# The SSM norm's factors leave the state-space stage's pools: one tile for the sum of squares and the broadcast factors

## The chip, the cores and the metric

The kernel runs on one core of a Trainium2 chip. The time is that of one execution on the device in microseconds. Of the kernel before, three runs gave 1232.15, 1234.88 and 1235.67 us (median 1234.88); one further execution, taken with the hardware profiler, took 1229.0 us.

The core has five engines with queues of their own that work in order: PE (TensorE, matrix products), DVE (VectorE), ACT (ScalarE), POOL (GpSimd), and SP, which here issues the transfers (DMA). Operands live in the on-chip SBUF, matrix products end in PSUM.

## The reference, cut to what matters

One layer of a hybrid decoder: 1024 positions of width 1024, a state-space branch and an attention branch over the same normalised input.

```
h = rmsnorm(x, norm_w) * (1 + scale) + shift
z_ssm, xbc, dt_raw, q, k, v, z_att, f_logit, g_logit = split(h @ w_in)
y_ssm = rmsnorm(ssd(xbc, dt_raw, ...) * silu(z_ssm), ssm_norm_w)     # 16 heads of 64, chunks of 128
y_att = softmax(q k^T * scale + f_cum_q - f_cum_k, causal) v * silu(z_att)   # 8 heads of 128
merged = sigmoid(g_ssm) * (y_ssm @ w_proj_ssm) + sigmoid(g_att) * (y_att @ w_proj_att)
out = rmsnorm(x + gate * (merged @ w_out), final_norm_w)
```

The change concerns the second `rmsnorm`: for each position the mean of the squares over the 1024 state-space channels, its inverse square root, and the product of that factor with the channels.

## The kernel before, in words

All large products are made from operands split into a high and a low part (`split`: a copy by ACT into `hi`, a subtraction by DVE into `lo`), with three partial products for each. Activations lie with channels on the 128 partitions and positions along the row, in eight tiles `hh[k]`, `hl[k]` of 128 x 1024.

After the normalisation and most projections comes the **state-space stage** (pools `sd` in SBUF on the right-hand side and `sdp` in PSUM). It runs over four groups of four heads (`qd`), two halves of the positions (`hf`) and four chunks in each (`ssd_half`). A chunk has a broadcast of decays (`ab`), transposes of the inputs, a state update (`sps`, `st32`, split into `sn`), the outputs in the chunk (`yd`) and those from the carried state (`yo`). After each half, DVE applies skip and gate, ACT squares, and DVE adds to `sacc`, a 128 x 1024 tile that in the end holds, per partition and position, the sum of squares over the channels of that partition. Projections that are independent of it (`FILL`: v, and q and k of several heads) are written between the groups, and the scheduler puts them into gaps on PE.

At the stage's end, eight matmuls with a column of ones add `sacc` over the partitions into `rps`; DVE scales into `rc`, POOL raises to the power -1/2, PE transposes into `rtp`, DVE copies into `rr`, and a DMA stores the 1024 factors in `r_scr`. `rps` and `rtp` are `sp` tiles of the stage's PSUM pool and `sacc` is a tile of its SBUF pool. Then a new pool `m0p` is opened, and a second DMA broadcasts the factors from `r_scr` to the 128 x 1024 tile `rb`. `u_scaled(j)` loads the state-space output `u_scr[j]`, multiplies by `rb` and the weight column, and stores it in `us_scr[j]` for the later projection.

The **attention stage** follows (pools `at` in SBUF, at the place of `sd`, and `atp` in PSUM, at the place of `sdp`): a pool's first tiles wait for the last readers of what lay there before. Before the loop over heads stand, in program order, one `u_scaled`, `qk_slab(0)` (q and k of head 0 are loaded and split) and `v_load(0)`. In head `h`, `attend` makes the logits `lg` for pairs of 128-row blocks, their exponential, transposes `tp`, the product with v in `pv`, and the next head's `qk_slab(h + 1)` is written behind it. For heads whose q or k was not projected earlier that means `c_slab`: two halves of 24 matmuls (lines 111 to 113), each into one tile `mm` of a ring of three that serves the whole program (`mm_tile`), evacuated into `qh`, `ql` or `kh`, `kl` of the pool `at`.

The order on each engine is set once, when the program is built, by a scheduler that plays the program through with its own costs: `attend` and `ssd_half` have raised priorities, and what has no raised priority is drawn ahead into gaps as far as buffers allow. Tiles of one ring are handed out in program order.

Of the kernel before, what the change touches and what calls it, by code (L numbers as in the profile page):

```python
# [24 lines left out]
F32 = mybir.dt.float32  # L25
# [6 lines left out]
P = 128  # L32
S = 1024
# [28 lines left out]
R_C, R_SHIFT, R_SCALE, R_NW, R_SNW, R_BG, R_CB, R_CW = 0, 8, 16, 24, 32, 40, 56, 66  # L62
# [3 lines left out]
def build(ctx, tc, t):  # L66
    nc = tc.nc
    V, A, G, PE, SP = nc.vector, nc.scalar, nc.gpsimd, nc.tensor, nc.sync
# [7 lines left out]
    def f32(ap):  # L76
        return ap.bitcast(F32)

    def ev(name):
        return evp.tile([P, 1028], F32, tag="ev", bufs=4, name=name)  # L80
# [16 lines left out]
    def split(raw, hi, lo, n, eng=V):  # L97
        A.copy(out=hi[:, :n], in_=raw[:, :n])  # L98
        eng.tensor_tensor(out=lo[:, :n], in0=raw[:, :n], in1=f32(hi[:, :n]), op=ALU.subtract)  # L99
        return hi, lo  # L100

    def mm_tile():
        return mmp.tile([P, 512], F32, tag="mm", name="mm")
# [11 lines left out]
    def c_slab(src, slab, xh, xl, evac):  # L115

        units = [unit(src[slab, u], 512) for u in range(2)]
        for hf in range(2):
            ps = mm_tile()
            c_half(hf, units, xh, xl, ps)  # L120
            evac(slice(hf * 512, (hf + 1) * 512), ps)
# [29 lines left out]
    cols = const.tile([P, NROWS], F32, name="cols")  # L151
# [7 lines left out]
    r_scr = dram.tile([8, P], F32, name="r_scr")  # L159
# [174 lines left out]
    def v_slab(pair, dtf=None):  # L334
        vt = []

        def evac(tb, ps):
            per = ps.shape[1]
            g, i = tb // 4, tb % 4
            if i == 0:  # L340
                vt.append(ev("vt")[:, :1024].rearrange("p (i c) -> p i c", i=4))
            A.copy(out=vt[g][:, i:i + per, :], in_=ps[:, :, 0:256])
            if dtf is not None:
                V.tensor_copy(out=dtf[:, tb:tb + per, :], in_=ps[:, :, 256:280])
            if i + per == 4:
                SP.dma_start(out=v_scr[pair][g], in_=vt[g])

        if dtf is not None:
            with tc.issue_after(was["last"].ins):
                t_slab([t["w_v0"][u] for u in range(4)], 280, hh, hl, evac)  # L350
        else:
            t_slab([t["w_v"][pair - 1, u] for u in range(4)], 256, hh, hl, evac)
# [274 lines left out]
            fb()  # L627


    with tc.tile_pool(name="sd", bufs=1, side="right") as sd, \  # L630
            tc.tile_pool(name="sdp", bufs=1, space=PSUM) as sdp:

        def sp():
            return sdp.tile([P, 512], F32, tag="sp", bufs=4, name="sp")
# [115 lines left out]
        def qk_spill(n, h):  # L750
            evac, store = qk_out(n, h)
            c_slab(t["w_c"], (Q0 if n == "q" else K0) + h, hh, hl, evac)
            store()

        fill = [lambda p=p: v_slab(p) for p in (1, 2, 3)] + [lambda a=a: qk_spill(*a) for a in SPILL]
        sacc = sd.tile([P, S], F32, name="sacc")
        for qd in range(4):
            st32, sn = sd.tile([P, 256], F32, tag="st32", bufs=1, name="st32"), None
            for hf in range(2):
# [7 lines left out]
                for i in range(2):  # L767
                    j = 2 * qd + i
# [10 lines left out]
                    SP.dma_start(out=u_scr[j][:, hs], in_=y)  # L779
            for f in FILL[qd]:  # L780
                fill[f]()
        rps = sp()
        for tb in range(8):
            PE.matmul(rps[:, 2 * tb:2 * tb + 1], lhsT=sacc[:, tb * P:(tb + 1) * P], rhs=ones[:, 0:1],
                      start=True, stop=True)
# [1 line left out]
        V.tensor_scalar(out=rc, in0=rps[:, 0:16].rearrange("p (a two) -> p a two", two=2)[:, :, 0],  # L787
                        scalar1=1.0 / 1024, scalar2=4 * EPS, op0=ALU.mult, op1=ALU.add)
        G.tensor_tensor(out=rc, in0=rc, in1=mhalf, op=ALU.pow)  # L789
        rtp = sp()  # L790
        PE.transpose(out=rtp[0:8, 0:P], in_=rc, identity=ident)
        rr = const.tile([8, P], F32, name="rr")
        V.tensor_copy(out=rr, in_=rtp[0:8, 0:P])
        SP.dma_start(out=r_scr, in_=rr)


    LO, HI = slice(0, 512), slice(512, 1024)
    rctx, finx = ExitStack(), ExitStack()
    m0p = rctx.enter_context(tc.tile_pool(name="m0p", bufs=1, side="right"))
    rb = m0p.tile([P, S], F32, tag="rb", bufs=1, name="rb")  # L800
    SP.dma_start(out=rb, in_=r_scr.rearrange("(o c) l -> o (c l)", o=1).broadcast_to([P, S]))

    def u_scaled(j):
        ut = ev("ut")
        SP.dma_start(out=ut[:, :S], in_=u_scr[j])
        V.scalar_tensor_tensor(out=ut[:, :S], in0=ut[:, :S], scalar=cols[:, R_SNW + j:R_SNW + j + 1], in1=rb,
                               op0=ALU.mult, op1=ALU.mult)
        SP.dma_start(out=us_scr[j], in_=ut[:, :S])

# [157 lines left out]
    with tc.tile_pool(name="at", bufs=1, side="right") as at, \  # L967
            tc.tile_pool(name="atp", bufs=1, space=PSUM) as atp:

        def qk_slab(h):  # L970
            qh, ql, kh, kl = (at.tile([P, S], F32R, tag=n, bufs=2, name=n) for n in ("qh", "ql", "kh", "kl"))
            def q_evac(hs, ps):
                A.activation(out=qh[:, hs], in_=ps, func=AF.Copy, scale=-QSCALE)
                V.scalar_tensor_tensor(out=ql[:, hs], in0=ps, scalar=-QSCALE, in1=f32(qh[:, hs]),
                                       op0=ALU.mult, op1=ALU.subtract)

            def k_evac(hs, ps):
                A.copy(out=kh[:, hs], in_=ps)
                V.tensor_tensor(out=kl[:, hs], in0=ps, in1=f32(kh[:, hs]), op=ALU.subtract)
            for n, slab, evac, hi, lo in (("q", Q0 + h, q_evac, qh, ql), ("k", K0 + h, k_evac, kh, kl)):  # L980
                if (n, h) in SPILL + PSPILL:
                    qt = ev("qt")
                    SP.dma_start(out=qt[:, :S], in_=qk_scr[n, h])
                    split(qt, hi, lo, S)
                else:
                    c_slab(t["w_c"], slab, hh, hl, evac)
            return qh, ql, kh, kl
# [6 lines left out]
        def v_load(pair):  # L994
            vh, vl = [], []
            for g in range(2):
                vt = ev("vt")[:, :1024].rearrange("p (i c) -> p i c", i=4)
                SP.dma_start(out=vt, in_=v_scr[pair][g])
                vh.append(at.tile([P, 4, 256], F32R, tag="vh", bufs=3, name="vh"))
                vl.append(at.tile([P, 4, 256], F32R, tag="vl", bufs=3, name="vl"))  # L1000
                split(vt, vh[g], vl[g], 4)
            return vh, vl
# [55 lines left out]
            SP.dma_start(out=o_scr[h], in_=zg[:, :S])  # L1058

        prep = iter(range(8))  # L1060
        for _ in range(PREP[-1]):
            u_scaled(next(prep))
        qkt = qk_slab(0)
        vv = v_load(0)
        for h in range(AH):
            if h == HCLOSE:
                hctx.close()
                fin = finx.enter_context(tc.tile_pool(name="fin", bufs=1))
            zg = z_load(h)
            with tc.high_priority(offset=APRI):  # L1070
                attend(h, qkt, vv, zg)
            if h < AH - 1:
                if h % 2:
                    vv = v_load((h + 1) // 2)
                qkt = qk_slab(h + 1)
            if h in EARLY:
                early(EARLY[h])
                if 1 in EARLY[h]:
                    ub = b_quads(us_scr, (12, 22))
            for _ in range(PREP[h]):  # L1080
                u_scaled(next(prep))
# [167 lines left out]
```

## Time and profile before

| | |
|---|---|
| three runs, median (lowest to highest) | 1234.88 us (1232.15 to 1235.67) |
| the profiled execution | 1229.0 us, its span 1227.2 us |
| PE busy | 1162.5 us, 95% of the span |
| DVE busy | 969.8 us, 79% |
| ACT busy | 626.2 us, 51% |
| POOL busy | 87.2 us, 7% |
| end of the last sum into `sacc` | 728.7 us |
| first logits of attention | 733.8 us |
| first multiplication by `rb` | 742.2 us |

Times within the span count from its start. Rows of single instructions show start, duration, engine, line, operation, and in brackets how long the engine stood idle before it and what ended that. Matmuls overlap: the distance from one start to the next is what one costs, its duration is longer. A row with "x8" stands for eight that follow each other, with the time they took together. The rows themselves are shown where the prediction uses them.

### The profile page before, as it was taken

How to read it: one execution, taken by the hardware profiler on the slowest of the kernel's cores; microseconds unless marked ns; L12 is line 12 of the kernel's file. 1: busy time of each engine (PE TensorE's matmuls, PEld its weight loads, DVE VectorE, ACT ScalarE, POOL GpSimd, SP SyncE). 2: the span in 40 equal slices, each digit the busy share in tenths (PEclk: the TensorE clock that was granted, in tenths of full speed). 3: DMA queues.
4: the chain of work that ended last, by engine and by line, in shares of the span. 5: the costliest groups of instructions: out<-in, count | busy, mean ns of one | idle time of the engine just before them, and what ended most of it. 6: DMA issues, size and time to landing. Idle time of an engine off the chain costs nothing.

```text
span 1227.2 us, 18314 instructions
## 1 busy us (share of the span) xinstructions
PE 1162.5 (95%) x6206; PEld 975.1 (79%) x6206; DVE 969.8 (79%) x1990; ACT 626.2 (51%) x1252; POOL 87.2 (7%) x152
## 2 busy tenths in 40 slices
PE   4999899999999999999999989999988998999997
PEld 3797688778877788998888768888877886788875
DVE  6879687887987785589999987664677968989967
ACT  5555344353442344777776633453456654454455
POOL 2000000000000000000000002222322220000001
PEclk9999999999999999999999989999999999999999
DMA  8442442655384756546646658422246526955333
GB/s 350 178 155 98 165 164 79 229 188 190 115 291 167 243 206 223 207 134 205 207 149 199 205 185 304 157 88 89 87 162 208 182 77 239 334 181 180 103 95 146
DMA packets 104122, 219.67 MB, mean 179 GB/s; under 512 B 11818, under 2 KB 19420, under 8 KB 103004
## 3 DMA queue, kind: packets, MB, share of 16 engines
q1 hardware_dynamic: 104028, 218.50, 52.8%
q8 instruction: 49, 0.80, 0.3%
q14 instruction: 45, 0.37, 0.1%
HBM read 154.85 MB, written 63.61 MB: 178 GB/s over the span
## 4 chain that ended last, share of the span: by engine, by line
PE 71%; DVE 14%; DMA 8%; issue 3%; ACT 3%; POOL 0%; SPq 0%; POOLq 0%; DVEq 0%; ACTq 0%
PE pp L492 6%; PE pp L495 6%; PE pp L494 6%; PE pv L1054 4%; PE mm L492 4%; PE mm L494 4%; PE mm L495 4%; PE lg L1023 3%; PE mm L112 3%; PE mm L111 3%; PE mm L113 3%; DMA ab<-a_scr 2%; PE tp L1044 2%; PE mm L908 2%; PE mm L906 2%
## 5 line engine op out<-in xcount | busy, mean ns | idle before, releaser
L98 ACT CAST wh<-wr 128x512 fp32r<-128x512 f32 (+1 forms) x214 | 130.4, 620 | 159.6 <-PE mm L494 27.9
L99 DVE TENSOR_TENSOR wl<-wr,wh 128x512 fp32r<-128x512 f32 (+1 forms) x214 | 145.8, 689 | 47.3 <-ACT wh L98 46.1
L112 PE MATMUL mm<-hl,wh 128*128 128x512 f32 x288 | 116.9, 406 | 0.0
L111 PE MATMUL mm<-hh,wh 128*128 128x512 f32 x288 | 115.5, 406 | 0.1
L113 PE MATMUL mm<-hh,wl 128*128 128x512 f32 x288 | 114.7, 399 | 0.0
L138 PE MATMUL mm<-wh,hl 128*128 128x256 f32 (+1 forms) x256 | 73.7, 289 | 0.0
L136 PE MATMUL mm<-wh,hh 128*128 128x256 f32 (+1 forms) x256 | 73.2, 288 | 0.0
L137 PE MATMUL mm<-wl,hh 128*128 128x256 f32 (+1 forms) x256 | 73.1, 286 | 0.0
L1029 ACT ACTIVATE pr<-pr,sm 128x1024 f32<-128x1024 f32 (+3 forms) x64 | 50.0, 781 | 44.9 <-DVE sm L1028 38.0
L1047 ACT CAST pth<-tp 128x512 fp32r<-128x512 f32 (+1 forms) x80 | 42.4, 542 | 52.7 <-PE tp L1044 44.1
L1024 DVE CUSTOM_DVE_ANT_0 pr<-lg,fb 128x512 f32<-128x512 f32 (+1 forms) x96 | 51.6, 552 | 17.8 <-PE lg L1023 12.2
L112 PEld LDWEIGHTS mm<-hl,wh 128*128 128x128 f32 x288 | 54.9, 191 | 10.8 <-DVE hl L303 0.9
L111 PEld LDWEIGHTS mm<-hh,wh 128*128 128x128 f32 x288 | 54.5, 191 | 10.9 <-ACT hh L302 0.9
L113 PEld LDWEIGHTS mm<-hh,wl 128*128 128x128 f32 x288 | 54.8, 190 | 10.1
L683 ACT ACTIVATE ab<-ab,acs 128x128 f32<-128x128 f32 x128 | 41.0, 391 | 36.5 <-DMA ab<-a_scr 32.7
L1032 POOL TENSOR_SCALAR pr<-pr,sm 128x1024 f32<-128x1024 f32 (+3 forms) x64 | 52.0, 813 | 83.1 <-DVE sm L1031 65.9
L1048 DVE TENSOR_TENSOR ptl<-tp,pth 128x512 fp32r<-128x512 f32 (+1 forms) x80 | 49.9, 631 | 10.0 <-ACT pth L1047 9.7
L789 POOL TENSOR_TENSOR rc<-rc,mhalf 128x8 f32<-128x8 f32 x1 | 1.6, 1647 | 703.9 <-DVE rc L787 703.9
L1054 PE MATMUL pv<-pth,vh 128*128 128x256 f32 (+1 forms) x160 | 45.2, 282 | 4.9 <-DVE zg L1057 4.0
L98 ACT CAST sh<-sr 128x512 fp32r<-128x512 f32 x57 | 34.0, 620 | 30.3 <-PE pp L494 15.0
L137 PEld LDWEIGHTS mm<-wl,hh 128*128 128x128 f32 x256 | 48.2, 189 | 0.2
L138 PEld LDWEIGHTS mm<-wh,hl 128*128 128x128 f32 x256 | 48.2, 189 | 0.1
(399 smaller groups left out, 3507.6 us busy)
## 6 DMA issues: line engine op xcount, KB each, us to landing
wr<-w_c SPq DMA_DIRECT2D x116, 256.0 KB, 3.4
wa<-w_ada SPq DMA_DIRECT2D x8, 1024.0 KB, 11.4
g_scr<-gt SPq DMA_DIRECT2D x16, 512.0 KB, 4.1
ab<-a_scr SPq DMA_DIRECT2D x32, 256.0 KB, 3.6
gt<-g_scr SPq DMA_DIRECT2D x32, 256.0 KB, 3.9
wr<-w_ps SPq DMA_DIRECT2D x28, 256.0 KB, 2.9
wr<-w_pa SPq DMA_DIRECT2D x28, 256.0 KB, 2.8
wr<-so SPq DMA_DIRECT2D x28, 256.0 KB, 2.7
```

Source lines behind the costliest of these rows:

```text
L98: A.copy(out=hi[:, :n], in_=raw[:, :n])
L99: eng.tensor_tensor(out=lo[:, :n], in0=raw[:, :n], in1=f32(hi[:, :n]), op=ALU.subtract)
L111: PE.matmul(ps, lhsT=hi[:, cs], rhs=xh[k][:, hs], start=(k == 0), stop=False)
L112: PE.matmul(ps, lhsT=hi[:, cs], rhs=xl[k][:, hs], start=False, stop=False)
L113: PE.matmul(ps, lhsT=lo[:, cs], rhs=xh[k][:, hs], start=False, stop=(k == 7))
L136: PE.matmul(o, lhsT=xh[k][:, ts], rhs=hi[:, cs], start=(k == 0), stop=False)
L137: PE.matmul(o, lhsT=xh[k][:, ts], rhs=lo[:, cs], start=False, stop=False)
L138: PE.matmul(o, lhsT=xl[k][:, ts], rhs=hi[:, cs], start=False, stop=(k == 7))
L492: PE.matmul(ps, lhsT=f[0][:, w], rhs=xh[:, hs], start=(first and k == 0), stop=False, skip_group_check=True)
L494: PE.matmul(ps, lhsT=f[0][:, w], rhs=xl[:, hs], start=False, stop=False, skip_group_check=True)
L495: PE.matmul(ps, lhsT=f[1][:, w], rhs=xh[:, hs], start=False, stop=(k == 3), skip_group_check=True)
L1054: PE.matmul(pv[:, o0:256], lhsT=x[kb // 4][:, kb % 4, vs], rhs=y[:, d:d + m], start=(kb == 0 and i == 0), stop=(kb == 2 * qq + 1 and i == 2))
```

## The change

`sacc` moves into `m0p`, which is now opened ahead of the state-space stage and stays until the factors are used. The computation of the factors becomes `norm_factors`, written behind `qk_slab(0)` and `v_load(0)`, outside the stage's pools; its two PSUM tiles are `mm` tiles. The factors are broadcast back into `sacc`, and `rb` is gone. The first `u_scaled` is written behind that.

```diff
+    rctx, finx = ExitStack(), ExitStack()
+    m0p = rctx.enter_context(tc.tile_pool(name="m0p", bufs=1, side="right"))
+    sacc = m0p.tile([P, S], F32, name="sacc")
 
     with tc.tile_pool(name="sd", bufs=1, side="right") as sd, \
...
-        sacc = sd.tile([P, S], F32, name="sacc")
         for qd in range(4):
...
-        rps = sp()
+
+    LO, HI = slice(0, 512), slice(512, 1024)
+    def norm_factors():
+        rps = mm_tile()
         for tb in range(8):
             PE.matmul(rps[:, 2 * tb:2 * tb + 1], lhsT=sacc[:, tb * P:(tb + 1) * P], rhs=ones[:, 0:1],
                       start=True, stop=True)
...
         G.tensor_tensor(out=rc, in0=rc, in1=mhalf, op=ALU.pow)
-        rtp = sp()
+        rtp = mm_tile()
         PE.transpose(out=rtp[0:8, 0:P], in_=rc, identity=ident)
         rr = const.tile([8, P], F32, name="rr")
         V.tensor_copy(out=rr, in_=rtp[0:8, 0:P])
         SP.dma_start(out=r_scr, in_=rr)
-
-
-    LO, HI = slice(0, 512), slice(512, 1024)
-    rctx, finx = ExitStack(), ExitStack()
-    m0p = rctx.enter_context(tc.tile_pool(name="m0p", bufs=1, side="right"))
-    rb = m0p.tile([P, S], F32, tag="rb", bufs=1, name="rb")
-    SP.dma_start(out=rb, in_=r_scr.rearrange("(o c) l -> o (c l)", o=1).broadcast_to([P, S]))
+        SP.dma_start(out=sacc, in_=r_scr.rearrange("(o c) l -> o (c l)", o=1).broadcast_to([P, S]))
 
     def u_scaled(j):
...
-        V.scalar_tensor_tensor(out=ut[:, :S], in0=ut[:, :S], scalar=cols[:, R_SNW + j:R_SNW + j + 1], in1=rb,
+        V.scalar_tensor_tensor(out=ut[:, :S], in0=ut[:, :S], scalar=cols[:, R_SNW + j:R_SNW + j + 1], in1=sacc,
...
         prep = iter(range(8))
+        qkt = qk_slab(0)
+        vv = v_load(0)
+        norm_factors()
         for _ in range(PREP[-1]):
             u_scaled(next(prep))
-        qkt = qk_slab(0)
-        vv = v_load(0)
```

Lines behind the stage's head shift by five at most: the sums over the partitions are line 784 before and 791 now, the transpose of the factors 791 and 798, the logits 1023 and 1024, the scaling 806 and 807.

Three places show how the scheduler's order moves. In the rows, `sp` and `mm` are PSUM tiles, `hh_231` to `hh_238` and `hl_239` to `hl_246` the eight tiles of the normalised input, and `wh`, `wl` a split weight.

TensorE at the end of the state-space stage, before: the last projections ahead of the sums, the transpose and the first logits.

```order
L111 MATMUL mm<-hh_238,wh 128x512
L112 MATMUL mm<-hl_246,wh 128x512
L113 MATMUL mm<-hh_238,wl 128x512
L784 MATMUL sp<-ones,sacc 128x1 x4
L791 MATMUL sp<-ident,rc 8x128
L1023 MATMUL lg<-kh,qh 128x512
L1023 MATMUL lg<-kl,qh 128x512
L1023 MATMUL lg<-kh,ql 128x512
```

The same place now:

```order
L733 MATMUL sp<-m_7147,xr 64x128 x12
L791 MATMUL mm<-ones,sacc 128x1 x4
L744 MATMUL sp<-ch_4525,sn 128x128
L745 MATMUL sp<-cl_4527,sn 128x128
L744 MATMUL sp<-ch_4525,sn 128x128
L745 MATMUL sp<-cl_4527,sn 128x128
L791 MATMUL mm<-ones,sacc 128x1 x4
L1024 MATMUL lg<-kh,qh 128x512 x2
L1024 MATMUL lg<-kl,qh 128x512
```

and a few rows on:

```order
L1024 MATMUL lg<-kl,qh 128x512
L1024 MATMUL lg<-kh,ql 128x512
L798 MATMUL mm<-ident,rc 8x128
L111 MATMUL mm<-hh_231,wh 128x512
L112 MATMUL mm<-hl_239,wh 128x512
L113 MATMUL mm<-hh_231,wl 128x512
```

Counted over the whole order, 72 of the 96 projection matmuls of head 1 stood ahead of the first logits, between the chunks of the last half; now none stands there, and the first one follows the transpose of the factors. Both orders have the same number of projections behind them again 216 projections after the first logits now (144 before).

VectorE at the same seam, before:

```order
L773 TENSOR_TENSOR ys<-ys,zt 128x512 x2
L778 TENSOR_TENSOR sacc<-sacc,zt 128x512 x2
L787 TENSOR_SCALAR rc<-sp 128x8
L99 TENSOR_TENSOR ql<-qt,qh 128x1024
L99 TENSOR_TENSOR kl<-qt,kh 128x1024
L793 COPY rr<-sp 8x128
L99 TENSOR_TENSOR vl<-vt,vh 128x1024
L974 SCALAR_TENSOR_TENSOR ql<-mm,qh 128x512 x2
L979 TENSOR_TENSOR kl<-mm,kh 128x512
L1024 ISA pr,sm<-lg,fb 128x512
```

and now:

```order
L782 TENSOR_TENSOR sacc<-sacc,zt 128x512 x2
L99 TENSOR_TENSOR ql<-qt,qh 128x1024
L794 TENSOR_SCALAR rc<-mm 128x8
L99 TENSOR_TENSOR kl<-qt,kh 128x1024
L99 TENSOR_TENSOR vl<-vt,vh 128x1024 x2
L1025 ISA pr,sm<-lg,fb 128x512
L1025 ISA sm 128x1
L1025 ISA pr,sm<-lg,fb 128x512
L1025 ISA sm 128x1
L800 COPY rr<-mm 8x128
```

`rc` moves behind the split of q, the copy `rr` behind two readouts of logits, and the three evacuations of head 1's projections (lines 974 and 979) leave this place. The first multiplication by the factors stands behind four readouts now, and behind two before.

TensorE in head 0, at its last logits, before and now:

```order
L1023 MATMUL lg<-kl,qh 128x128
L1023 MATMUL lg<-kh,ql 128x128
L1054 MATMUL pv<-pth,vh 128x256
L1054 MATMUL pv<-pth,vl 128x256
L1054 MATMUL pv<-ptl,vh 128x256
```

```order
L1024 MATMUL lg<-kh,ql 128x128
L111 MATMUL mm<-hh_233,wh 128x512
L112 MATMUL mm<-hl_241,wh 128x512
L113 MATMUL mm<-hh_233,wl 128x512
L111 MATMUL mm<-hh_234,wh 128x512
L112 MATMUL mm<-hl_242,wh 128x512
```

Sixteen projections stand now between these logits and the product with v, where none stood.

## The prediction

> **What bounds the kernel now.** I read four views in this order: the engine shares and the chain that ended last, a table by stage around the place of the change, the instructions of TensorE and VectorE there, and the waits.
>
> From the page of the profile, the first two shares and the chain:
>
> ```profile
> span 1227.2 us, 18314 instructions
> PE 1162.5 (95%) x6206; PEld 975.1 (79%) x6206; DVE 969.8 (79%) x1990; ACT 626.2 (51%) x1252; POOL 87.2 (7%) x152
> PE 71%; DVE 14%; DMA 8%; issue 3%; ACT 3%; POOL 0%; SPq 0%; POOLq 0%; DVEq 0%; ACTq 0%
> ```
>
> TensorE works 1162.5 of 1227.2 us. All matmuls are the same before and after, so the question is only where its 64.7 us of idle time grow or shrink. By stage (the columns are length, busy time and count of PE, weight loads, DVE, ACT, POOL, then granted clock, DMA share, GB/s):
>
> ```profile
> 702.00:727.00 25.00, 24.43 (x155) 20.13 (x153) 24.14 (x59) 8.42 (x18) 0.00 (x0) 1.00 0.44 143
> 727.00:736.50 9.50, 4.13 (x16) 3.21 (x16) 7.00 (x11) 5.21 (x8) 2.23 (x3) 0.65 0.72 254
> 736.50:798.00 61.50, 59.11 (x327) 50.88 (x326) 41.25 (x98) 25.23 (x49) 14.41 (x23) 1.00 0.66 230
> 798.00:880.00 82.00, 81.90 (x497) 72.25 (x495) 48.33 (x138) 39.33 (x83) 22.46 (x41) 1.00 0.26 91
> 880.00:960.00 80.00, 73.24 (x418) 62.54 (x416) 58.87 (x153) 44.20 (x88) 22.32 (x36) 0.98 0.47 159
> ```
>
> The last stretch of the state-space stage (702 to 727) has DVE at 24.14 of 25 us: it is set by VectorE, and TensorE is full as well, at 24.43. The seam (727 to 736.5) leaves PE over half idle. After it attention is set by TensorE: 59.11 of 61.5, then 81.90 of 82 us, with DVE at two thirds or less. What fills TensorE in the DVE-bound tail is shown by the largest of its groups there (there are three alike, one for each partial product):
>
> ```profile
> L111 PE MATMUL mm<-hh,wh 128*128 128x512 f32 x25 | 10.0, 400 | 0.0
> ```
>
> They are projections of head 1's q and k, which belong to attention and run here for nothing, under VectorE.
>
> **The change part by part.** The factors' two PSUM tiles move from the stage's own pool into the ring of three `mm` buffers, which those projections use too, and stand in it ahead of head 1. The order shows what comes of it: before, 72 of head 1's 96 projection matmuls stand ahead of the first logits; now none does, they begin only behind the transpose of the factors. Counting the projections on TensorE, both orders are even again after the 144 that follow the first logits before (about 798 us), which become 216. No arithmetic is added or removed.
>
> *Cover lost.* The price of one such matmul is its distance to the next when they stand back to back, not its modelled duration:
>
> ```profile
> 707.38 0.39 PE L111 MATMUL mm<-hh,wh 128*128 128x512 f32 x1
> ...
> 710.15 0.39 PE L111 MATMUL mm<-hh,wh 128*128 128x512 f32 x1
> ```
>
> Between these two lie twelve steps in 2.77 us, 0.231 us each. 72 x 0.231 = 16.6 us of TensorE work leave a stretch where they cost nothing and land in one where TensorE is full. That is +16.6 us, unless holes take it up.
>
> *The tail itself.* Does it end sooner? Its VectorE queue:
>
> ```profile
> 717.64 0.68 DVE L99 TENSOR_TENSOR wl<-wr,wh 128x512 fp32r<-128x512 f32 x1
> 718.36 0.42 DVE L741 TENSOR_TENSOR ys<-sp,eb 128x256 f32<-128x256 f32 x1
> ...
> 720.63 0.69 DVE L99 TENSOR_TENSOR wl<-wr,wh 128x512 fp32r<-128x512 f32 x1
> 721.35 0.42 DVE L99 TENSOR_TENSOR sn<-st,sn 64x256 fp32r<-64x256 f32 x1
> 721.80 0.42 DVE L741 TENSOR_TENSOR ys<-sp,eb 128x256 f32<-128x256 f32 x1
> 722.26 0.85 DVE L744 TENSOR_TENSOR ys<-sp,ys 64x256 f32<-64x256 f32 x2
> ...
> 727.25 1.49 DVE L778 TENSOR_TENSOR sacc<-sacc,zt 128x512 f32<-128x512 f32 x2
> ```
>
> The two weight splits (0.72 us each by the next start) go to attention, since the projections no longer free their buffers: -1.4 us at most. Against that, the last state split `sn` now stands right ahead of the multiplication `L741` that needs its matmuls; before, 1.3 us of other work lay between (721.80 to 723.14). I give back 0.9 us for that round trip and take -0.5 us. Bounds: -1.4 us, and +3 us if TensorE, now mostly idle here, answers at half rate (below). Behind the lost cover nothing else hides the tail's wait: TensorE simply stands.
>
> *The seam.* Before, qh's split and the first logits wait for the factors:
>
> ```profile
> 728.79 1.05 PE L784 MATMUL sp<-ones,sacc 128*128 128x1 f32 x8 [2.18 <-DVE sacc L778]
> 731.82 0.38 PE L791 MATMUL sp<-ident,rc 128*8 128x128 f32 x1 [1.99 <-POOL rc L789]
> 733.80 0.77 PE L1023 MATMUL lg<-kh,qh 128*128 128x512 f32 x1 [1.60 <-DMA fb<-f_scr]
> 736.50 0.49 PE L111 MATMUL mm<-hh,wh 128*128 128x512 f32 x1
> 730.12 1.65 POOL L789 TENSOR_TENSOR rc<-rc,mhalf 128x8 f32<-128x8 f32 x1 [703.91 <-DVE rc L787]
> 730.07 1.04 ACT L98 CAST qh<-qt 128x1024 fp32r<-128x1024 f32 x1 [2.26 <-DVE rc L787]
> 731.15 1.23 DVE L99 TENSOR_TENSOR ql<-qt,qh 128x1024 fp32r<-128x1024 f32 x1 [1.11 <-ACT qh L98]
> 732.29 1.22 DVE L99 TENSOR_TENSOR kl<-qt,kh 128x1024 fp32r<-128x1024 f32 x1
> 733.43 0.27 DVE L793 COPY rr<-sp 8x128 f32<-8x128 f32 x1
> ```
>
> The tail's sums end at 728.74. The logits start at 733.80, right behind the copy `rr` (733.70), the last reader of the stage's PSUM pool: 5.06 us, of which 1.05 + 0.38 are work, so 3.6 us idle. Now the pools close with the tail, at T. qh is split T to T+1.0 and kh to T+2.1 on ACT, ql to T+2.3 and kl to T+3.6 on DVE (with `rc` in between); the first two logit matmuls can start at T+2.1, the others at T+3.6. Work in that time is 1.05 us and two logit matmuls of 0.45 (six took 733.80 to 736.50), so TensorE is idle about 1.6 us: -2.0 us. The factor chain moves behind the logits: pow done at T+4.2, transpose at T+6, the copy after two logit readouts at T+7.7. Bounds 0 (another load, such as fb's, still decides) and -3.3 us, the lead that the second logit readout gets.
>
> *The moved scaling.* The broadcast and the `u_scaled` multiplications behind it get later:
>
> ```profile
> 733.90 0.33 SPq L794 DMA_DIRECT2D r_scr<-rr x1
> 738.54 0.32 SPq L801 DMA_DIRECT2D rb<-r_scr x1
> 742.16 2.48 DVE L806 SCALAR_TENSOR_TENSOR ut<-ut,cols,rb 128x1024 f32<-128x1024 f32 x2 [1.94 <-DMA rb<-r_scr]
> ```
>
> From the copy's end to the first multiplication it was 8.5 us (733.7 to 742.16), so it now starts at T+16.2 instead of 13.4 us after the tail. VectorE reaches it after four logit readouts, near T+12, and stands 4 us. Behind it wait block 6's minimum, its exponential, two more multiplications, q's evacuation and the reciprocal; the probabilities are ready about T+22. TensorE comes to their transposes after 64 projections (64 x 0.231 = 14.8) and twelve logit matmuls (2.3) from T+6, at T+23. So I price it at nothing: the projections hide it, with 1 us to spare; without the cover it costs those 4 us. On SP the w_c loads of later heads now queue behind the `us_scr` stores, but q1, k1 and the first half of q2 are split in the tail already, so no projection starves.
>
> *Holes that take the work.* Between 736.5 and 798 TensorE waits once, and later for VectorE:
>
> ```profile
> PE pv L1054 <- DVE zg L1057: 2.2, 1, 2.2
> PE lg L1023 <- DVE sm L1024: 4.0, 3, 2.9
> ```
>
> The first (at 772) lies between head 0's last logits and its values; 16 projections now stand there, 3.7 us, so it fills: -2.2 us. The others lie past 880, behind the point where both orders agree; the work ahead of them moves as one, so they stay.
>
> **The sum:** +16.6 - 0.5 - 2.0 - 2.2 = +11.9 us on the profiled execution's 1229.0 us (span 1227.2), 1240.9. The median of the runs, 1234.88, is 5.9 us above that execution; I add the difference to it: 1246.8, and name 1246.5.
>
> A rule of the Trainium skill speaks against the change as well. The row first: the clock was 0.65 over the seam, and its logit matmuls took 0.45 us each against 0.231. "TensorE: Matmul & The Clock Gate", Part 1, says that half rate is the default and that roughly a 3.4 us window of activity lifts it. The trace agrees in size (2.7 us slow); whether a sparse tail counts as idle no row shows. By the rule the sum would be that of the second rival.
>
> **The rivals.** (1) *Faster.* If attention is set not by TensorE but by the chain of logits, exponential and values, its earlier start carries to the end: -3.3 at the seam and -0.5 in the tail, 1231. For it: the seam's wait is real. Against it: 81.90 of 82 us busy, and one wait of TensorE from 736.5 to 880. It decides only if the 72 matmuls find holes: 16.6 us, where the rows show 2.2 before 880 and 6.8 to 960. Chance 5%. (2) *A slow tail.* Without projections the tail has 24.43 - 16.6 = 7.8 us of matmuls in 25. If its clock falls to half, as at the seam, the groups that VectorE waits for double:
>
> ```profile
> 716.45 0.52 PE L711 MATMUL sp<-xr,bt 128*128 128x256 f32 x3
> 716.80 0.88 PE L728 MATMUL sp<-m,xr 128*64 128x128 f32 x12
> ...
> 721.54 0.88 PE L728 MATMUL sp<-m,xr 128*64 128x128 f32 x12
> 722.25 0.27 PE L739 MATMUL sp<-ch,sn 128*128 128x128 f32 x1
> ```
>
> States take 0.35, outputs 0.71 and the carried part some 0.45 us (four matmuls of the same kind), by their starts: 1.5 us more a chunk, half of it exposed over four chunks, +3. It decides from the point where VectorE has gaps. If the scaling also stands in the way, +4 more: 1250 to 1254. Chance 20%. (3) *Later holes take part.* If half the 6.8 us idle of 880 to 960 is a fixed cost of loads, the sum falls to +8: 1243 or less; with all of it and the clean tail, +4: 1239. Chance 20%. (4) *Nothing moves*, all holes and the seam together cancel the cover: 1235. Chance 5%. The forecast has 50%.
>
> **How the numbers follow.** The range takes the forecast, rival 3 and most of rival 2: 1239 to 1253. This kernel's runs tell 0.3%, 3.7 us, from no change. Faster is rival 1, 5%; same is rival 4 and the lowest tenth of 3, 7%; slower the rest, 88%.
>
> **What would show it.** After the change TensorE should be near 35% busy in the last 25 us of the state-space stage, with no projection ahead of the first logits, and busy without pause from there past the end of head 1. The first logits should start 2 to 3.6 us behind the last `sacc` sum; the first scaling 16 us behind it. The forecast is wrong if TensorE has idle time in heads 0 to 2 that a trace of before doesn't show, or if the tail shrinks by more than 2 us.

## The result, and the profile after

The changed kernel's median over five runs is 1244.27 us (1242.27 to 1249.23), against 1235.67 us (1232.15 to 1237.89) for the kernel before in the same session: a ratio of 1.008, 95% interval 1.0057 to 1.0102. That is 7.0 to 12.6 us more. In a second session the unaltered change gave 1248.14 against 1236.65, ratio 1.0096 (1.007 to 1.0122).

The profiled execution of the change took 1249.23 us, with a span of 1247.5. Some 6 us of that had already gathered ahead of the place of the change, compared with the first profile of before. So the stretches below are shifted by 6.5 us, and the parts are compared from landmark to landmark.

The table by stage after the change (length, then busy time and count of PE, weight loads, DVE, ACT, POOL, then granted clock, DMA share, GB/s): the last 25 us of the state-space stage, the seam, the first 10 us of logits, then the rest to the point where both orders agree, and beyond.

```profile
708.50:733.50 25.00, 13.10 (x83) 11.28 (x81) 22.58 (x57) 6.96 (x16) 0.00 (x0) 0.60 0.37 122
733.50:738.20 4.70, 1.87 (x8) 1.78 (x8) 2.58 (x4) 2.98 (x5) 0.00 (x0) 0.50 0.52 159
738.20:748.20 10.00, 9.66 (x30) 7.08 (x31) 5.53 (x12) 3.12 (x4) 5.15 (x5) 0.70 0.78 295
748.20:821.00 72.80, 71.74 (x399) 61.73 (x398) 45.03 (x104) 28.94 (x59) 14.97 (x26) 1.00 0.53 188
821.00:900.00 79.00, 79.00 (x467) 69.49 (x466) 45.80 (x127) 36.00 (x75) 19.91 (x36) 1.00 0.26 91
```

The tail has 83 matmuls where it had 155, TensorE is busy in half of it instead of all, and its clock has fallen to 0.60. VectorE is still nearly full. Attention is full on TensorE as before. The groups of TensorE in the same tail show what is left: the state-space matmuls and, of the 25 projections of each kind, one at its start (lines 733, 744 and 745 are 728, 739 and 740 before; lines of the stage shift by up to five, those of the norm's factors by seven):

```profile
L733 PE MATMUL sp<-m,xr 128*64 128x128 f32 x48 | 5.4, 289 | 3.3 <-DVE st L722 3.3
L744 PE MATMUL sp<-ch,sn 128*128 128x128 f32 x8 | 3.1, 395 | 4.8 <-DVE sn L99 4.8
L745 PE MATMUL sp<-cl,sn 128*128 128x128 f32 x8 | 3.0, 381 | 0.0
L111 PE MATMUL mm<-hh,wh 128*128 128x512 f32 x1 | 0.4, 444 | 0.0
```

The seam after, by instruction of TensorE, ACT and VectorE:

```profile
735.45 1.87 PE L791 MATMUL mm<-ones,sacc 128*128 128x1 f32 x8 [5.68 <-DVE sacc L782]
738.24 1.22 PE L1024 MATMUL lg<-kh,qh 128*128 128x512 f32 x2 [0.92 <-ACT kh L98]
741.63 0.41 PE L798 MATMUL mm<-ident,rc 128*8 128x128 f32 x1
741.70 0.78 PE L111 MATMUL mm<-hh,wh 128*128 128x512 f32 x1
736.19 1.04 ACT L98 CAST qh<-qt 128x1024 fp32r<-128x1024 f32 x1 [1.72 <-DMA u_scr<-ys]
729.80 0.42 DVE L746 TENSOR_TENSOR ys<-sp,eb 128x256 f32<-128x256 f32 x1 [1.67 <-PE sp L745]
733.91 1.49 DVE L782 TENSOR_TENSOR sacc<-sacc,zt 128x512 f32<-128x512 f32 x2
743.13 0.27 DVE L800 COPY rr<-mm 8x128 f32<-8x128 f32 x1
751.79 1.28 DVE L807 SCALAR_TENSOR_TENSOR ut<-ut,cols,sacc 128x1024 f32<-128x1024 f32 x1 [2.10 <-DMA sacc<-r_scr]
```

The sums end at 735.40, the logits start 2.84 us later (before: 5.06), and the first projection follows the transpose of the factors, as its order says. TensorE waits in the tail for VectorE's states (4.8 + 3.3 us) and 5.68 us for the last sum.

A second profile of each kernel was taken later. The table gives, for every profiled execution that follows, the stretches between five landmarks: U, the second square that starts a sum (before anything the change moves); E, the start of the last addition to `sacc`; G, the first logits; F, the last matmul of line 111, which belongs to the last projections; and the end of the span. The starts come from the groups of these tiles in each trace.

| us | U to E | E to G | G to F | F to end | U to end |
|---|---|---|---|---|---|
| before, first profile | 143.1 | 5.8 | 176.9 | 316.5 | 642.3 |
| before, second profile | 145.5 | 5.7 | 179.3 | 317.2 | 647.7 |
| change, first profile | 143.9 | 3.5 | 193.1 | 316.2 | 656.7 |
| change, second profile | 144.4 | 3.5 | 192.3 | 317.1 | 657.3 |
| tiles in attention's ring | 142.8 | 4.3 | 178.1 | 318.0 | 643.2 |
| before, with mm tiles | 145.5 | 10.6 | 187.6 | 317.0 | 660.7 |
| factors behind head 1 | 145.2 | 4.2 | 184.9 | 317.6 | 651.9 |
| before, one tile | 144.5 | 5.8 | 180.7 | 317.3 | 648.3 |
| change, 72 matmuls left out | 143.6 | 3.6 | 178.3 | 316.7 | 642.2 |
| before, 72 matmuls left out | 144.6 | 6.4 | 174.3 | 317.0 | 642.3 |
| change, 72 matmuls added | 145.2 | 3.5 | 191.6 | 317.2 | 657.5 |

The loss stands in one column: from the first logits to the last projection the change takes 13 to 16 us more, the seam gives back 2.2, and the two other columns differ by no more than they do among executions of one kernel.

### The profile page after: what moved, and what is told of

Its sections match the earlier page's. It is cut to its first block, busy times and chain, and to the rows that moved or that the text cites. A ratio compares the mean times of both kernels' runs of the same rounds, so it can differ in the third digit from the quotient of the medians.

```text
span 1247.5 us, 18316 instructions
## 1 busy us (share of the span) xinstructions
PE 1173.9 (94%) x6206; PEld 983.7 (79%) x6206; DVE 972.7 (78%) x1990; ACT 626.6 (50%) x1252; POOL 87.9 (7%) x152
## 4 chain that ended last, share of the span: by engine, by line
PE 45%; DVE 11%; DMA 8%; ACT 3%; issue 2%; SPq 0%; POOL 0%; POOLq 0%; DVEq 0%; ACTq 0%
PE pv L1055 4%; DMA ab<-a_scr 3%; PE lg L1024 3%; PE mm L111 2%; PE mm L112 2%; PE mm L113 2%; PE tp L1045 2%; PE pp L492 2%; PE pp L494 2%; PE pp L495 2%; PE mm L907 2%; PE mm L909 2%; PE mm L908 2%; PE pp L909 1%; PE pp L1167 1%
## 5 line engine op out<-in xcount | busy, mean ns | idle before, releaser
L136 PEld LDWEIGHTS mm<-wh,hh 128*128 128x128 f32 x256 | 48.1, 189 | 0.2
```

Of the source, the lines that this page charges most:

```text
L136: PE.matmul(o, lhsT=xh[k][:, ts], rhs=hi[:, cs], start=(k == 0), stop=False)
```

## The experiments

**The unaltered kernels again**, for second profiles.

> The changed kernel unaltered, for a second profile beside those of its variants. Cover theory: +7 to +13 us against before; the 6.5 us that the first profile was already late before the first instruction that the change moves are chance of that execution and differ here.

Measured: 1248.14 us, ratio 1.0096 (1.007 to 1.0122). The landmark U came at 590.8 us in the first profile of the change and at 589.1 in the second, against 584.9 and 586.6 for before: over all executions of the table above it lies between 584.9 and 590.8, although TensorE's order is the same up to there. The lateness goes with the clock at the program's start. From 20 to 150 us, first profile of before, then of the change:

```profile
20.00:150.00 130.00, 120.76 (x626) 100.37 (x626) 106.80 (x237) 65.12 (x115) 2.43 (x4) 1.00 0.46 165
20.00:150.00 130.00, 119.38 (x606) 99.53 (x607) 105.88 (x235) 62.74 (x111) 2.44 (x4) 0.97 0.45 163
```

In this stretch the clock was 1.00 in the four executions with U at 584.9 to 587.3, and 0.96 or 0.97 in the seven with U at 588.3 to 590.8. One of the seven is the kernel before with mm tiles, whose pools are untouched, so the lateness is taken as chance of the execution and left out by counting from U. That the change has no part in it is not shown: all six executions of versions made from the change are among the seven.

> The kernel before unaltered, for a second profile. The first one was taken from an execution of 1229.0 us, below all timed runs of it. From one landmark ahead of the change (the second square that starts a sum, at 584.9 us) to the end it took 642.3 us, and the one-tile variant, whose TensorE order is the same, 648.3. If that execution was a quick one, this one takes 644 to 650 from the landmark, and the surplus lies in waits of attention or in its clock; if it was typical, 641 to 643.

Measured: from the landmark to the end 647.7 us. The first profile of before was a quick execution, as this expectation supposed. Of the 5.4 us, 2.4 lie in U to E, whose cause stays open, and 2.4 in G to F. For the latter one cause can be seen here (a second, the clock behind the seam, is shown further on). In both profiles TensorE waits about 2 us in head 0 for VectorE (`pv` for `zg`). In the first the clock stays up behind the hole, in the second it does not. The stages of 10 us behind the hole, first profile, then second:

```profile
773.80:783.80 10.00, 10.00 (x55) 8.49 (x55) 7.00 (x16) 4.52 (x10) 1.84 (x4) 1.00 0.50 182
```

```profile
777.80:787.80 10.00, 10.00 (x49) 8.79 (x48) 6.42 (x15) 3.53 (x8) 1.42 (x4) 0.83 0.46 175
```

**One thing undone: the factors' tiles in another ring.**

```diff
-        rps = mm_tile()
+        rps = atp.tile([P, 512], F32, tag="tp", bufs=2, name="tp")
...
-        rtp = mm_tile()
+        rtp = atp.tile([P, 512], F32, tag="tp", bufs=2, name="tp")
```

> The changed kernel with one thing undone: the two PSUM tiles of the factors come from attention's ring for transposes instead of the mm ring. All 72 projections of head 1 stand ahead of the first logits again. Cover theory: the loss is gone and the earlier seam stays, 0 to 4 us faster than before (about -2), so 8 to 14 us faster than the change. Rival, the scaling by the factors in VectorE's way: it is as late as in the change, so most of the loss stays, +5 us or more against before. Rival, the place of the one tile in SBUF or the longer-lived pool: +6 us stay.

Measured: 1232.21 us against 1237.96, ratio 0.9962 (0.9945 to 0.9979): 2.6 to 6.8 us faster than before. With the projections back in the tail the whole loss is gone, although the scaling still starts 15.1 us behind the last sum (16.4 in the change) and the tile is the same. TensorE's tail is nearly full again, and the stretch of head 0 in which before has its hole shows none:

```profile
708.50:733.50 25.00, 22.52 (x142) 19.05 (x140) 22.30 (x51) 6.67 (x14) 0.00 (x0) 0.96 0.47 154
765.40:775.40 10.00, 10.00 (x64) 8.94 (x63) 7.74 (x16) 6.13 (x14) 2.65 (x5) 1.00 0.79 295
```

This version beats both kernels. Its gain over before, 4.7 us by the ratio, is a little above the 0 to 4 expected. Against the second profile the table shows 1.4 us of it at the seam and 1.2 in G to F; 2.7 lie in U to E, which differs by as much among executions. The hole is gone from G to F, but TensorE waits 1.0 us there for the evacuation of `ql`, and the half rate of the seam goes on for 9.8 us behind the first logits.

**One part alone: mm tiles in the kernel before.**

```diff
-        rps = sp()
+        rps = mm_tile()
...
-        rtp = sp()
+        rtp = mm_tile()
```

> The kernel before with one part of the change alone: the two PSUM tiles of the factors are mm tiles; everything else, the pools, the place in the program and the two SBUF tiles, as before. Cover theory: the tail has no projections again, 18 come between the transpose of the factors and the first logits; the seam keeps its old waits. 72 x 0.231 = 16.6 us, less 18 x 0.231 = 4.2 us that may fit into the seam's wait and less 2.2 us for the hole in head 0: +8 to +14 us against before. Rivals (scaling, place of the tile): those parts are as before, so 0 to +2 us.

Measured: 1248.1 us, ratio 1.0099 (1.0075 to 1.0122), +9 to +15 us. These two lines alone make the loss, without any of the rest of the change. TensorE waits as long for the last sum as in the change, and then for the factors as before:

```profile
PE mm L784 <- DVE sacc L778: 5.7, 1, 5.7
PE mm L791 <- POOL rc L789: 2.0, 1, 2.0
```

**The other part alone: one tile for sum and factors.**

```diff
+    rctx, finx = ExitStack(), ExitStack()
+    m0p = rctx.enter_context(tc.tile_pool(name="m0p", bufs=1, side="right"))
+    sacc = m0p.tile([P, S], F32, name="sacc")
...
     with tc.tile_pool(name="sd", bufs=1, side="right") as sd, \
...
-        sacc = sd.tile([P, S], F32, name="sacc")
...
-    rctx, finx = ExitStack(), ExitStack()
-    m0p = rctx.enter_context(tc.tile_pool(name="m0p", bufs=1, side="right"))
-    rb = m0p.tile([P, S], F32, tag="rb", bufs=1, name="rb")
-    SP.dma_start(out=rb, in_=r_scr.rearrange("(o c) l -> o (c l)", o=1).broadcast_to([P, S]))
+    SP.dma_start(out=sacc, in_=r_scr.rearrange("(o c) l -> o (c l)", o=1).broadcast_to([P, S]))
...
-        V.scalar_tensor_tensor(out=ut[:, :S], in0=ut[:, :S], scalar=cols[:, R_SNW + j:R_SNW + j + 1], in1=rb,
+        V.scalar_tensor_tensor(out=ut[:, :S], in0=ut[:, :S], scalar=cols[:, R_SNW + j:R_SNW + j + 1], in1=sacc,
```

> The kernel before with the other part of the change alone: one tile, outside the stage's pool, for the sum of squares and for the broadcast factors; the computation of the factors stays where it was, with the stage's PSUM tiles. TensorE's order is as before. Cover theory: within 1 us of before. Rival, the tile's place: +3 to +8 us.

Measured: 1238.5 us, ratio 1.0019 (1.0002 to 1.0036), 0.2 to 4.5 us more. That is not the loss, but it is not clearly nothing either; the profile (648.3 us from the landmark, 647.7 in the second of before) shows no place for it, and at 1236.02 us it is one of the quickest of its twelve executions. Neither the expected 1 us nor the lower end of the rival's 3 to 8 us is excluded. Against the rival speaks that the version with the tiles in attention's ring has the same tile and is quicker than before. It stays open.

**The factors behind head 1's projections.**

```diff
         vv = v_load(0)
-        norm_factors()
-        for _ in range(PREP[-1]):
-            u_scaled(next(prep))
         for h in range(AH):
...
+            if h == 0:
+                norm_factors()
+                u_scaled(next(prep))
             for _ in range(PREP[h]):
```

> The changed kernel with the factors written behind head 1's projections instead of ahead of them, so that their two mm tiles come later in the ring. 72 projections stand ahead of the logits again, the factors come some 20 us later still. Cover theory: -1 to -4 us against before, as with the other ring, whatever the factors' lateness. Rival, late scaling: slower than the change, +10 us or more against before.

Measured: 1242.32 us, ratio 1.004 (1.0023 to 1.0058). The expectation missed: the cover is back, and it is still slower than before, though faster than the change; the rival's +10 us is not reached either. Here the late scaling does hurt. VectorE stands for the broadcast and for the loads, and what it owes attention comes late; TensorE waits and its clock falls behind that. VectorE's waits from 758 to 790 us, one such scaling ahead of the split `ptl` that TensorE waits for, the wait of TensorE, and the stage of 10 us around it:

```profile
DVE ut L807 <- DMA ut<-u_scr: 5.3, 2, 3.2
DVE ut L807 <- DMA sacc<-r_scr: 2.6, 1, 2.6
```

```profile
781.02 1.28 DVE L807 SCALAR_TENSOR_TENSOR ut<-ut,cols,sacc 128x1024 f32<-128x1024 f32 x1 [2.03 <-DMA ut<-u_scr]
782.96 0.39 PE L1055 MATMUL pv<-ptl,vh 128*128 128x256 f32 x1 [2.74 <-DVE ptl L1049]
```

```profile
778.20:788.20 10.00, 7.25 (x41) 6.52 (x40) 6.02 (x14) 4.30 (x9) 1.23 (x4) 0.83 0.88 281
```

The idle 2.74 us and about 1.7 us for the clock (0.83 over 10 us) account for 4.4 of the 6.8 us by which its G to F is longer than with the other ring; the remaining 2.4 were not traced.

**The disputed cost itself: 72 matmuls taken away.** In both kernels, head 1's q and k sum 6 of 24 partial products, so that 72 of the 96 projection matmuls are missing.

```diff
-    def c_half(hf, units, xh, xl, ps):
+    def c_half(hf, units, xh, xl, ps, ks=range(8)):
...
-        for k in range(8):
+        for k in ks:
...
     def c_slab(src, slab, xh, xl, evac):
+        ks = (0, 7) if slab in (Q0 + 1, K0 + 1) else range(8)
...
-            c_half(hf, units, xh, xl, ps)
+            c_half(hf, units, xh, xl, ps, ks)
```

> The changed kernel without 72 of the 96 projection matmuls of head 1 (its q and k are left incomplete: 6 of each 24 partial products are summed). Cover theory: TensorE sets attention, so 72 x 0.231 = 16.6 us less, of which 2.2 are lost again as the hole in head 0 opens: 12 to 17 us faster than the change, about 2 to 6 us faster than before. Rival, attention set by the chain of logits, exponential and values: 0 to 5 us faster than the change.

> The kernel before without the same 72 matmuls (the same 6 of 24 are summed). They stood in the tail that VectorE sets. Cover theory: they were free there, so within 3 us of before (a little faster if their queue delayed the chunks, a little slower if TensorE's clock falls). Rival, the tail is set by TensorE as much as by VectorE: 8 to 16 us faster than before.

Measured: the change without them 1234.31 us, ratio to before 0.9978 (0.9962 to 0.9995); the kernel before without them 1234.18, ratio 0.9989 (0.9972 to 1.0007). The same matmuls are worth 1.0096 - 0.9978 = 1.2%, 14.6 us, in the change, and nothing that can be measured in the kernel before. One reservation: of the 72 only 54 were missing in the tail there, and 18 behind the first logits, where they should have given 4.2 us; the table has G to F at 174.3, 5.0 shorter than in the second profile, and 0.7 us lost again at the seam. In this version, too, the clock fell in the tail (0.68 over its last 25 us), and U to E, at 144.6, lies between the two profiles of before.

**The cover put back with idle work.** Ahead of the factors' tiles in the ring stand three mm tiles, filled with 72 matmuls that nobody reads.

```diff
+        cov = unit(t["w_c"][Q0, 0], 512)
+        for i in range(3):
+            ps = mm_tile()
+            for k in range(24):
+                PE.matmul(ps, lhsT=cov[0][:, (k % 4) * P:(k % 4 + 1) * P], rhs=hh[k % 8][:, LO], start=(k == 0),
+                          stop=(k == 23))
         qkt = qk_slab(0)
         vv = v_load(0)
         norm_factors()
```

> The changed kernel with 72 matmuls more, whose results nobody reads, in three mm tiles ahead of the factors' tiles (and one more weight load and split for them). They stand in the tail. Cover theory: 16.6 us of added work cost nothing there; they keep TensorE's clock up, which takes 1 to 3 us off: -3 to +1 us against the change. Rival, the tail slows by TensorE's half clock and that is most of the loss: 5 us or more faster than the change. Rival, TensorE sets the tail: 5 us or more slower than the change.

Measured: 1246.07 us, ratio to before 1.008 (1.0054 to 1.0107), beside 1.0096 for the change in the same session. 16.6 us of added TensorE work cost nothing, so the tail is VectorE's. TensorE is full there again and its clock up:

```profile
708.50:733.50 25.00, 23.08 (x151) 19.62 (x150) 23.39 (x56) 7.96 (x17) 0.00 (x0) 1.00 0.43 138
```

With TensorE kept busy there the time is at most a little better, so the half clock in the tail is not what the loss consists of.

## Why the prediction was right

It forecast +11.9 us, slower, by the projections that lose their cover. Both measurements, +8.6 and +11.5 by the medians, lie near it, and the runs bear out the mechanism: the ring alone makes the loss, another ring takes it away, and the matmuls are free in one place and cost about 0.2 us each in the other. How near the number came is in part luck: from U to the end the four profiles of the two kernels give +9.0 to +15.0 us.

*Cover lost, +16.6, and the hole filled, -2.2.* Together +14.4 for G to F. Against the first profile of before it is +15.4 to +16.2, against the second +13.0 to +13.8. The hole at the end of head 0 is gone, as forecast. What was missed: in an execution where that hole also drops the clock it is worth 2 us plus about 1.7, not 2.2 alone. The term for the hole is too small for such an execution, and the sum was made from one in which the hole was cheap. The clock behind the seam had no term at all. The stretches from the first logits to the end of the half rate, first and second profile of before, then of the change:

```profile
733.80:736.70 2.90, 2.90 (x7) 2.33 (x8) 2.90 (x5) 0.67 (x2) 0.58 (x2) 0.50 1.04 410
737.84:744.00 6.16, 6.16 (x15) 4.81 (x16) 5.28 (x10) 1.71 (x3) 0.68 (x2) 0.50 0.74 297
738.24:744.30 6.06, 5.76 (x13) 3.92 (x14) 5.33 (x11) 2.54 (x3) 4.03 (x4) 0.50 0.99 366
737.00:741.57 4.57, 4.26 (x10) 2.72 (x11) 4.57 (x8) 1.85 (x2) 3.73 (x3) 0.50 0.94 337
```

At half rate at most half of such a stretch is lost. The change then loses up to 1.6 and 0.8 us more here than the first profile of before, about what it has above +14.4 there. This is an estimate from these rows; no run tests it alone.

*The tail, -0.5.* Not resolved. U to E differs by 2.7 us among executions, and the change lies in the middle. The two splits are gone from it; the round trip that was given back at 0.9 us shows as a wait of 1.67 us before `L746`, with the carried part's matmuls at half rate.

*The seam, -2.0.* Measured -2.2 to -2.3, by a path that was read wrongly in one point: qh's split does not start with the last sum but 0.8 us later, when the store `u_scr<-ys` has read its tile; the row of ACT names it. Logits at T+2.84 instead of T+2.1.

*The scaling, nothing.* It started 16.4 us behind the last sum (16.2 forecast), and TensorE came to the first transposes without a wait. Only further on one wait for POOL appears that wasn't foreseen, in both profiles of the change and in neither of before. By the prediction's own sign, no new idle time in heads 0 to 2, it counts against the forecast; it is small beside the 16.6 us:

```profile
791.98 0.55 PE L1045 MATMUL tp<-ident,pr 128*128 128x128 f32 x3 [1.06 <-POOL pr L1033]
```

That this term was near its edge shows in the variant with still later factors, where it costs.

*The rivals.* The faster one fell: taking 72 matmuls out of attention gives 14.6 us. Of the slow tail the clock came true (0.60, then 0.50 at the seam), so TensorE was busy in 52% of the tail and not in the 35% named; but its price did not, since VectorE had other work in hand except for the 1.67 us. Later holes took no part: F to end is 316.2 and 317.1 against 316.5 and 317.2, and of the idle time between 880 us and F, 1.1 us before, as much is left in the same place now.

## What to carry to other kernels

Before a small piece of work gets buffers of a ring, look at who stands behind it in that ring: where tiles are handed out in program order, two short-lived tiles that wait for a late result can hold back everything that would have been drawn ahead. Work that one engine does under the cover of another costs its full time once it is moved to where its own engine is the bound, even though no busy total changes. And when a sum is made from one profiled execution, take a second one where TensorE has holes of some 2 us in an otherwise full stretch.

## What the runs showed of the hardware that was not expected

A hole of 1.97 us in an otherwise full TensorE stretch came just ahead of a fall of its clock. In the second profile of before, in stretches of one or more us:

```profile
776.96 0.36 PE L1054 MATMUL pv<-pth,vh 128*128 128x256 f32 x1 [1.97 <-DVE zg L1057]
```

```profile
776.00:779.00 3.00, 2.01 (x12) 1.84 (x12) 3.00 (x7) 1.71 (x4) 0.59 (x1) 0.86 0.41 149
779.00:780.00 1.00, 1.00 (x7) 1.00 (x6) 0.54 (x3) 0.02 (x1) 0.29 (x1) 0.50 0.20 78
780.00:781.00 1.00, 1.00 (x6) 1.00 (x5) 0.00 (x0) 1.00 (x2) 0.00 (x0) 0.50 0.00 0
781.00:782.00 1.00, 1.00 (x4) 0.77 (x4) 0.94 (x1) 1.00 (x4) 0.00 (x0) 0.72 0.00 0
782.00:783.00 1.00, 1.00 (x6) 0.79 (x5) 1.00 (x5) 0.40 (x3) 0.00 (x0) 1.00 0.00 0
```

The clock was 0.50 there and back at 1.00 by 782. The time at half rate adds up from twice what is missing to 1.00 in each stretch: 0.8 + 1.0 + 1.0 + 0.6 = 3.4 us. In the first profile a hole of 2.25 us at the same place left it at 1.00 (the row from 773.80 us, further up):

```profile
772.09 0.36 PE L1054 MATMUL pv<-pth,vh 128*128 128x256 f32 x1 [2.25 <-DVE zg L1057]
```

The Trainium skill, "TensorE: Matmul & The Clock Gate", Part 1, has the half rate follow an idle window of about 3.4 us; here shorter holes sufficed in two of the three executions with this TensorE order (the third, the one-tile variant, lost its clock behind 2.49 us), so by the measurement holes of 2 us already carry that risk. On the return the page and the trace agree, at those 3.4 us.

What may decide it is where the hole lies. In every trace of this case the clock changes only at times that are whole multiples of 3.41 us apart. Each trace can so be cut into steps of 3.41 us. In the first profile (two rows) the hole is divided between two steps; in the second (two rows) it lies wholly in one, and the clock is 0.50 in the next:

```profile
767.42:770.83 3.41, 2.42 (x23) 2.28 (x21) 0.74 (x4) 1.62 (x5) 0.96 (x2) 1.00 0.66 238
770.83:774.25 3.42, 2.13 (x16) 1.95 (x17) 3.42 (x8) 2.01 (x5) 0.59 (x1) 1.00 0.48 131
774.72:778.13 3.41, 1.42 (x10) 1.10 (x10) 2.94 (x6) 2.99 (x7) 0.59 (x1) 1.00 0.18 56
778.14:781.55 3.41, 3.41 (x16) 3.26 (x15) 1.89 (x5) 1.57 (x3) 0.29 (x1) 0.50 0.27 108
```

In the one-tile variant the step ahead of the fall had 1.20 us busy. No run tests this reading, and the busy share does not divide sharply: a step with 1.53 us busy kept the clock (398.25 us, before without the 72 matmuls), one with 1.75 lost it (699.59 us, one tile).

And in the change the thinned tail, busy in half its time, ran at 0.60 (the first stage row after the change). The clock fell there at 713.58 us, behind a step with 1.43 us busy, whose longest hole was 1.83 us:

```profile
712.63 0.30 PE L744 MATMUL sp<-ch,sn 128*128 128x128 f32 x1 [1.83 <-DVE sn L99]
710.17:713.58 3.41, 1.43 (x14) 1.08 (x13) 3.30 (x9) 2.42 (x6) 0.00 (x0) 1.00 0.16 51
713.58:716.99 3.41, 2.26 (x15) 1.78 (x15) 3.33 (x10) 0.40 (x1) 0.00 (x0) 0.50 0.69 230
```

So a stretch that is half busy, with no hole over 2.2 us, can lose the clock, which the prediction could not tell.
